# Ordering small TensorE products behind later dense products in a two-layer hybrid decoder: state-space last blocks and factors, delta-rule state updates and value transposes

## Chip, cores and metric

One Trainium2 chip, of which this kernel uses one core. The metric is the device time of the whole kernel in microseconds (us). Before the change three runs gave 2291.3 to 2293.06 us, with a median of 2291.31 us.

## What is computed

Two decoder layers over 512 tokens of width 1024, all in float32. Each layer projects the normalised input once, feeds three branches from it, and merges them:

```
y_ssd = ssd_mixer(ssd_z, ssd_xbc, ssd_dt, ...)          # 2 groups of 8 heads, blocks of 128 tokens
y_mla = mla_mixer(mla_cq, mla_ckv, mla_kr, ...)
y_gdn = gdn_mixer(gdn_qkv, gdn_z, gdn_b, gdn_a, ...)    # 8 value heads, state 128 x 128 each
mixed = g_ssd * (y_ssd @ w_ssd_out) + g_mla * (y_mla @ w_mla_out) + g_gdn * (y_gdn @ w_gdn_out)
h = x + mixed @ w_out
x = h + square(relu(rmsnorm(h) @ w_up)) @ w_down
```

Two parts matter here. The state-space mixer ends with `y * silu(z)` and an RMSNorm over the 512 channels of a group, so every token needs the sum of squares of its group before it gets a factor. The gated delta rule walks over the tokens block by block with a running state:

```
v_new = u - w @ state
o     = (q * exp(g)) @ state + qk @ v_new
state = state * exp(g_last) + (k * exp(g_last - g)).T @ v_new
```

## The kernel before

**Dense products.** Everything large is a product of 128x128 weights with 128x512 activations. An fp32 operand is split into a high and a low half, and `mm3` (L200 to L202) issues three matmuls for each product: high by high, and the two mixed ones. Weights arrive by DMA as `wraw` (two buffers), ScalarE casts them to `whi` (L172) and VectorE subtracts to get `wlo` (L173). `dense_F` runs over pairs of weight tiles k = 0..7 and over two output halves j = 0, 1, so one half-product of k is three matmuls; it accumulates in the PSUM banks called `acc`. Smaller products and transposes use three PSUM banks called `sm`, and one bank called `yt`.

**What sets the order.** Each engine runs its instructions in one fixed order, which a scheduler makes at build time. The kernel steers it with a pair of functions. `dense_F` registers every half-product under a key, `place((tag, k, j), end)`; `behind(key, ins)` puts a small product `ins` after that dense half-product. It is an order on TensorE only, without a semaphore. A key is, for example, `((ly, 1, 2 * g, "y"), 6, 0)`: in layer ly, branch 1 (latent attention), pair 2g of its output projection, the "y" half (attention output times its weights; "g" is the gate half before it), k = 6, j = 0.

**State-space group.** `ssd_group(g)` is built ahead of the output projection of latent attention for pairs 2g and 2g + 1, and its small products lie between those dense ones. For each token block t = 0..3 there are eight products of head width 64 (L784), for t > 0 four with the running state (L795), then VectorE adds (L788, L796, L797), multiplies by the gate (L811), ScalarE squares (L813), VectorE folds the squares (L814, L815), and one 128x1 product sums them over the partitions into the bank `yt` (L816). After t = 3 the factor is made: L277 on VectorE, a power on GpSimd (L278), a transpose on TensorE (L820), a copy (L822), and two DMAs through DRAM that spread it over the partitions (L823, L825). L829 multiplies it in.

**Delta-rule unit.** `gdn_unit(u)` does four heads; u = 0 runs while the projections of unit 1 go on, that is the keys `(ly, "k", 2)` and the values `(ly, "v", 4)` and `(ly, "v", 6)`; u = 1 runs in the output projection of the delta rule. For each token block: key by query (L1044), key by state (L1055), L1058 on VectorE, the inverse applied (L1061), VectorE's `vn` (L1066) and ScalarE's four scaled copies (L1072), the state update of two matmuls (L1075, into `pS`) followed by L1078 or L1082, then the outputs (L1085, L1092), L1093 and L1095, squares (L1101), and a norm with a power on GpSimd (L1105 to L1110, L278), multiplied in at L1113. At the end the unit's output is transposed in four pieces c (L1118) into the single bank `yt`, which L273 (ScalarE) and L274 (VectorE) read. In between lie the values: conv and SiLU (L719, L723, L281, L282), transposes (L1024) and L1025, and the keys' transposes (L1013, copied by L1014).

Of the kernel before, what the change touches and what calls it, by code (L numbers as in the profile page):

```python
# [20 lines left out]
P = 128  # L21
# [34 lines left out]
def hybrid_kernel(ctx, tc, a, out, depth=2, taps=None):  # L56
# [326 lines left out]
    for ly in range(depth):  # L383
# [350 lines left out]
        def ssd_group(g, yh, yl):  # L734
# [34 lines left out]
            for t in range(T):  # L769
# [11 lines left out]
                for c in range(4):  # L781
                    for i in range(2):
                        h = 2 * c + i
                        x = pe.matmul(py[64 * i : 64 * i + 64, c * P : (c + 1) * P], xd[:, t, h * 64 : (h + 1) * 64], e2[h // 4][:, h % 4, :], start=True, stop=True)  # L784
                        if t == 0:
                            behind(((ly, 1, 2 * g, "g"), 2, 0), x)
                y = xf[:, :, tok]
                dve.tensor_tensor(y, y, c4(py), ALU.add)  # L788
                if t > 0:
# [23 lines left out]
                act.activation(sq, zt, AF.Square)  # L813
                dve.tensor_tensor(sq[:, 0:2], sq[:, 0:2], sq[:, 2:4], ALU.add)  # L814
                dve.tensor_tensor(sq[:, 0], sq[:, 0], sq[:, 1], ALU.add)  # L815
                pe.matmul(pss[:, t : t + 1], sq[:, 0], ones[:, 0:1], start=True, stop=True)  # L816
            rs = mk(sp, [P, T], F32, "srs")
            rsq(rs, pss[:, :T], 1.0 / 512, EPS)
            ps = sm_bank()
            behind(((ly, 1, 2 * g, "y"), 6, 0), pe.transpose(ps[:T, :P], rs, ident))  # L820
            rsT = mk(br, [T, P], F32, "gk", 2)
            act.copy(rsT, ps[:T, :P])  # L822
            sync.dma_start(d_r[g].rearrange("(t p) -> t p", p=P), rsT)  # L823
# [172 lines left out]
        def gdn_unit(u, kT, ork, cc, cd, Yt, yh, yl):  # L996
# [20 lines left out]
            for i in range(2):  # L1017
                for j, pj in enumerate(dense_F(weights(w_in, O_GV + (4 * u + 2 * i) * P, 256, D), tiles(256), D, xh, xl, tag=(ly, "v", 4 * u + 2 * i))):
                    h = 2 * i + j
                    vf = mk(br, [P, S], F32, "ft4", 2)  # L1020
                    gconv_silu(pj, 8 + 4 * u + h, vf)
                    ps = sm_bank()
                    for t in range(T):
                        pe.transpose(ps[:, t * P : (t + 1) * P], vf[:, t * P : (t + 1) * P], ident)  # L1024
                    dve.tensor_tensor(v[:, :, h * P : (h + 1) * P], ps.rearrange("p (t n) -> p t n", t=T),  # L1025
                                      bc_last(ork[:, i, :], P), ALU.mult)
            silu_T(br, O_GZ + 512 * u, gz)
# [2 lines left out]
            ss = mk(sp, [P, T, 4], F32, "gos", 2)  # L1030
            g_, y_ = ((ly, 2, i // 2, "gy"[i % 2]) for i in range(2))
            seq = [(ly, "k", 2), (ly, "v", 4), (ly, "v", 6)] if u == 0 else [g_, y_, (ly, 2, 1, "g")]
            pw_place = (seq[0], 3, 0), (seq[0], 5, 1), (seq[1], 1, 0)
            pg_place = (seq[0], 5, 0), (seq[0], 7, 1)
            end_place = (seq[2], 1, 0) if u == 0 else (seq[2], 5, 0)
            st = None
            for t in range(T):
                tok = slice(t * P, (t + 1) * P)
# [29 lines left out]
                if t < T - 1:  # L1068
                    vd = mk(br, [P, 512], F32, "wk2")
                    for h in range(4):  # L1070
                        with tc.high_priority():
                            act.activation(hv(vd)[:, h], hv(pw)[:, h], AF.Copy, scale=cd[:, t, h : h + 1])  # L1072
                    pS = sm_bank()
                    for i in range(2):
                        pe.matmul(pS[:, i * 256 : (i + 1) * 256], ktok[i][:, t, :], vd[:, i * 256 : (i + 1) * 256], start=True, stop=True)  # L1075
                    sn = mk(br, [P, 512], F32, "st", 2)
                    if t == 0:
                        act.copy(sn, pS)  # L1078
                    else:
                        for h in range(4):  # L1080
                            with tc.high_priority():
                                dve.scalar_tensor_tensor(hv(sn)[:, h], hv(st)[:, h], hdec(2, t, h), hv(pS)[:, h], ALU.mult, ALU.add)  # L1082
                po = sm_bank()
                for h in range(4):
                    x = pe.matmul(po[:, h * P : (h + 1) * P], pt_[:, h, :], vn[:, h * P : (h + 1) * P], start=True, stop=True)  # L1085
                    if t == T - 1:
                        behind((seq[1], 1, 1), x)
                o = mk(br, [P, 512], F32, "wk3")
                if t > 0:
                    pq = sm_bank()  # L1090
# [370 lines left out]
```

## Time and profile before

| | |
|---|---|
| median of three runs | 2291.31 us |
| the profiled execution, its own time | 2290.89 us |
| its span in the trace | 2289.1 us |
| TensorE clock granted | 0.998 |
| GpSimd busy | 58.7 us |
| DMA, mean over the span | 107 GB/s |

Times inside the span are counted from its start. A row of the timeline gives the start, the length, engine, line and operation, the tile written, the tiles read, and how many instructions were merged; a square bracket behind it is the idle time of the engine before, with what ended it. Matmuls are pipelined and their ends are modelled, so two rows overlap; the distance from start to start is what counts. An fp32 matmul shows as two passes, so "x2" is one product and "x16" is eight. Rows of waits give the waiting engine and line, what it waited for, the total, the count and the longest.

### The profile page before, as it was taken

Reading aid. Unit: us, or ns where it says so; the run is one execution under the profiler, and the core shown is the slowest. Engines: PE = TensorE matmul, PEld = TensorE weight load, DVE = VectorE, ACT = ScalarE, POOL = GpSimd, SP = SyncE. Lnnn points to the kernel's source line nnn. Section 1 sums busy time; section 2 is a strip of 40 time slices with the busy share of each in tenths; the row PEclk is TensorE's granted clock in tenths of the full one; section 3 lists DMA queues with packets and bytes.
Section 4 is the critical chain, followed back from the end, with each engine's and each line's share of the span. In section 5 each row is a group of like instructions: output and inputs, shape, how many; then the busy total and the mean of one; then the engine's idle time right before and its main releaser. Section 6 shows DMA issues by size and latency. Waiting matters only on the chain.

```text
span 2289.1 us, 32304 instructions
## 1 busy us (share of the span) xinstructions
PE 2264.0 (99%) x11822; PEld 1866.7 (82%) x11822; DVE 1647.4 (72%) x3258; ACT 1202.8 (53%) x2508; POOL 58.7 (3%) x75
## 2 busy tenths in 40 slices
PE   9999999999999999999999999999999999999998
PEld 8888787888878888888888887878888887888886
DVE  7776567876676778767867775668757667778668
ACT  6766744333444465554657667443335435645545
POOL 0000000000000000000000000000001000000000
PEclk9999999999999999999999999999999999999999
DMA  4223633452225143233132236344422241432231
GB/s 144 81 74 102 193 102 120 123 150 76 77 74 172 59 148 111 92 109 105 52 100 78 77 104 199 96 119 140 129 76 82 65 170 52 166 108 99 89 111 47
DMA packets 220176, 244.23 MB, mean 107 GB/s; under 512 B 34272, under 2 KB 172528, under 8 KB 220016
## 3 DMA queue, kind: packets, MB, share of 16 engines
q1 hardware_dynamic: 220016, 242.16, 34.6%
q8 instruction: 93, 1.52, 0.3%
q14 instruction: 67, 0.55, 0.1%
HBM read 225.66 MB, written 11.74 MB: 104 GB/s over the span
## 4 chain that ended last, share of the span: by engine, by line
PE 91%; DVE 3%; ACT 2%; POOL 1%; DMA 1%; issue 0%; DVEq 0%; POOLq 0%; ACTq 0%; SPq 0%
PE acc L200 23%; PE acc L202 23%; PE acc L201 23%; PE sm L200 3%; PE sm L202 3%; PE sm L201 3%; DVE wlo L173 1%; PE sm L784 1%; PE sm L682 1%; PE sm L1085 1%; PE sm L1075 1%; PE yt L698 1%; ACT whi L172 1%; PE sm L662 1%; PE sm L659 0%
## 5 line engine op out<-in xcount | busy, mean ns | idle before, releaser
L173 DVE TENSOR_TENSOR wlo<-wraw,whi 128x512 fp32r<-128x512 f32 (+1 forms) x536 | 365.0, 686 | 344.0 <-ACT whi L172 333.8
L172 ACT CAST whi<-wraw 128x512 fp32r<-128x512 f32 (+1 forms) x536 | 329.5, 618 | 534.0 <-PE acc L201 367.1
L200 PE MATMUL acc<-xh,whi 128*128 128x512 f32 (+1 forms) x1344 | 524.5, 391 | 0.0
L201 PE MATMUL acc<-xl,whi 128*128 128x512 f32 (+1 forms) x1344 | 521.8, 388 | 0.0
L202 PE MATMUL acc<-xh,wlo 128*128 128x512 f32 (+1 forms) x1344 | 519.8, 387 | 0.0
L202 PEld LDWEIGHTS acc<-xh,wlo 128*128 128x128 f32 x1344 | 252.5, 188 | 48.8
L200 PEld LDWEIGHTS acc<-xh,whi 128*128 128x128 f32 x1344 | 252.5, 188 | 48.1 <-ACT xh L273 0.4
L201 PEld LDWEIGHTS acc<-xl,whi 128*128 128x128 f32 x1344 | 253.1, 188 | 47.3 <-DVE xl L274 0.7
L172 ACT CAST whi<-wr 128x512 fp32r<-128x512 f32 x168 | 104.3, 621 | 107.9 <-PE acc L201 47.7
L200 PE MATMUL acc<-yh,whi 128*128 128x512 f32 x384 | 151.5, 398 | 0.0
L201 PE MATMUL acc<-yl,whi 128*128 128x512 f32 x384 | 150.8, 393 | 0.0
L202 PE MATMUL acc<-yh,wlo 128*128 128x512 f32 x384 | 150.4, 392 | 0.0
L173 DVE TENSOR_TENSOR wlo<-wr,whi 128x512 fp32r<-128x512 f32 x168 | 113.2, 686 | 35.5 <-ACT whi L172 34.7
L723 DVE SCALAR_TENSOR_TENSOR ckl<-acc,pc,ckl 128x511 f32<-128x511 f32 (+2 forms) x168 | 121.1, 744 | 20.7 <-ACT ckl L719 13.0
L200 PEld LDWEIGHTS acc<-yh,whi 128*128 128x128 f32 x384 | 71.5, 188 | 16.7 <-ACT yh L273 2.3
L202 PEld LDWEIGHTS acc<-yh,wlo 128*128 128x128 f32 x384 | 72.2, 188 | 14.6
L201 PEld LDWEIGHTS acc<-yl,whi 128*128 128x128 f32 x384 | 72.2, 188 | 14.1
L200 PE MATMUL acc<-whi,xh 128*128 128x512 f32 (+1 forms) x208 | 79.9, 386 | 0.0
L201 PE MATMUL acc<-wlo,xh 128*128 128x512 f32 (+1 forms) x208 | 79.1, 380 | 0.0
L202 PE MATMUL acc<-whi,xl 128*128 128x512 f32 (+1 forms) x208 | 78.7, 381 | 0.0
L486 ACT ACTIVATE eE<-eE,cum 128x128 f32<-128x128 f32 x192 | 62.6, 391 | 28.6 <-DMA eE<-d_c 24.5
L1201 DVE TENSOR_TENSOR h<-h,acc 128x512 f32<-128x512 f32 x120 | 77.0, 680 | 0.1
(462 smaller groups left out, 4535.6 us busy)
## 6 DMA issues: line engine op xcount, KB each, us to landing
wraw<-in_w_in_dram SPq DMA_DIRECT2D x144, 512.0 KB, 3.6
wraw<-in_w_up_dram SPq DMA_DIRECT2D x64, 512.0 KB, 3.6
wr<-in_w_down_dram SPq DMA_DIRECT2D x32, 1024.0 KB, 5.3
eE<-d_c SPq DMA_DIRECT2D x48, 256.0 KB, 4.4
wraw<-in_w_mla_out_dram SPq DMA_DIRECT2D x16, 512.0 KB, 4.4
eE<-d_e SPq DMA_DIRECT2D x32, 256.0 KB, 3.1
wraw<-in_w_ssd_out_dram SPq DMA_DIRECT2D x16, 512.0 KB, 3.3
wraw<-in_w_gdn_out_dram SPq DMA_DIRECT2D x16, 512.0 KB, 3.4
```

Source lines behind the costliest of these rows:

```text
L172: act.copy(hi, raw)
L173: dve.tensor_tensor(lo, raw, f32(hi), ALU.subtract)
L200: pe.matmul(o, ah, bh, start=start, stop=False, skip_group_check=more)
L201: pe.matmul(o, ah, bl, start=False, stop=False, skip_group_check=more)
L202: return pe.matmul(o, al, bh, start=False, stop=stop, skip_group_check=more)
L486: act.activation(o[:, i], o[:, i], AF.Relu, scale=-1.0, bias=cum[:, t, h0 + i : h0 + i + 1])
L662: pe.matmul(o, qps[j][:, tok], kps[:, :n], start=False, stop=False)
L682: pe.transpose(ps[:, n : n + P], pn[t][:, kb * P : (kb + 1) * P], ident)
L698: pe.matmul(o, v_h, th[:, c : c + w], start=kb == 0, stop=False)
L723: dve.scalar_tensor_tensor(acc[:, d:], ps[:, : S - d], taps_[3 - d], acc[:, d:], ALU.mult, ALU.add)
L784: x = pe.matmul(py[64 * i : 64 * i + 64, c * P : (c + 1) * P], xd[:, t, h * 64 : (h + 1) * 64], e2[h // 4][:, h % 4, :], start=True, stop= ...
L1201: dve.tensor_tensor(hs_, hs_, ps[t], op)
```

## The change

Only orders are added or moved. (a) The last block's L784 products of a state-space group stand behind k = 3 of the projection 2g. (b) The sums L816 of t = 2 and t = 3 stand behind k = 3 and k = 7 there. (c) The factor's transpose L820 moves from k = 6 of that product to k = 1 of the gates of pair 2g + 1. (d) In `gdn_unit` for u = 1, the transposes of the first two value heads stand behind k = 5 of `(ly, "v", 6)`. (e) In both units the inverse's products (`pw_place`), the key-by-query products (`pg_place`) and the last outputs move to later dense products; the state updates of t = 1 and 2 get places of their own (`ps_place`); and the transposes that end unit 0 move from k = 1 to k = 7 of `(ly, "v", 6)`.

```diff
-                        if t == 0:
-                            behind(((ly, 1, 2 * g, "g"), 2, 0), x)
+                        if t in (0, T - 1):
+                            behind(((ly, 1, 2 * g, "g"), 2, 0) if t == 0 else ((ly, 1, 2 * g, "y"), 3, 0), x)
...
-                pe.matmul(pss[:, t : t + 1], sq[:, 0], ones[:, 0:1], start=True, stop=True)
+                x = pe.matmul(pss[:, t : t + 1], sq[:, 0], ones[:, 0:1], start=True, stop=True)
+                if t > 1:
+                    behind(((ly, 1, 2 * g, "y"), 4 * t - 5, 0), x)
...
-            behind(((ly, 1, 2 * g, "y"), 6, 0), pe.transpose(ps[:T, :P], rs, ident))
+            behind(((ly, 1, 2 * g + 1, "g"), 1, 0), pe.transpose(ps[:T, :P], rs, ident))
...
-                        pe.transpose(ps[:, t * P : (t + 1) * P], vf[:, t * P : (t + 1) * P], ident)
+                        x = pe.transpose(ps[:, t * P : (t + 1) * P], vf[:, t * P : (t + 1) * P], ident)
+                        if u == 1 and i == 0:
+                            behind(((ly, "v", 6), 5, j), x)
...
-            pw_place = (seq[0], 3, 0), (seq[0], 5, 1), (seq[1], 1, 0)
-            pg_place = (seq[0], 5, 0), (seq[0], 7, 1)
-            end_place = (seq[2], 1, 0) if u == 0 else (seq[2], 5, 0)
+            pw_place = (seq[0], 3, 0), (seq[0], 7, 0), (seq[1], 2, 0)
+            pg_place = (seq[0], 5, 1), (seq[1], 0, 1)
+            ps_place = (seq[0], 5, 0), (seq[1], 0, 0)
+            end_place = (seq[2], 7, 0) if u == 0 else (seq[2], 5, 0)
...
-                        pe.matmul(pS[:, i * 256 : (i + 1) * 256], ktok[i][:, t, :], vd[:, i * 256 : (i + 1) * 256], start=True, stop=True)
+                        x = pe.matmul(pS[:, i * 256 : (i + 1) * 256], ktok[i][:, t, :], vd[:, i * 256 : (i + 1) * 256], start=True, stop=True)
+                        if t > 0:
+                            behind(ps_place[t - 1], x)
...
-                        behind((seq[1], 1, 1), x)
+                        behind((seq[1], 2, 1), x)
```

In the changed kernel the same statements carry other line numbers from L818 on: L820 is there L822, L1024 is L1026, L1025 is L1029, L1075 is L1080, L1085 and L1092 are L1092 and L1099, L1110 and L1113 are L1117 and L1120, and L1118 is L1125.

**State-space group 0 of layer 0 on TensorE.** The rows are matmuls in their order, with the tile written, the tiles read and the size; L200 to L202 are dense. Here is the last block before the change:

```order
L201 MATMUL acc_3063<-yl_243_1066,whi_3066 128x512
L816 MATMUL yt_2695<-ct_75,wk_651_2839 128x1
L202 MATMUL acc_3063<-yh_242_1065,wlo_3067 128x512
L200 MATMUL acc_3062<-yh_326_1392,whi_3082 128x512
L784 MATMUL sm_2864<-eE_2844,tok_2256 64x128 x4
L795 MATMUL sm_2877<-ckh_547_2259,st_2835 128x128
L784 MATMUL sm_2864<-eE_2845,tok_2256 64x128 x4
L795 MATMUL sm_2877<-ckh_547_2259,st_2835 128x128 x3
L201 MATMUL acc_3062<-yl_327_1393,whi_3082 128x512
```

and here are the same products in the changed kernel:

```order
L201 MATMUL acc_3062<-yl_353_1493,whi_3082 128x512
L202 MATMUL acc_3062<-yh_352_1492,wlo_3083 128x512
L816 MATMUL yt_2695<-ct_75,wk_651_2839 128x1
L784 MATMUL sm_2864<-eE_2844,tok_2256 64x128 x4
L784 MATMUL sm_2864<-eE_2845,tok_2256 64x128 x4
L795 MATMUL sm_2877<-ckh_547_2259,st_2835 128x128 x4
L200 MATMUL acc_3063<-yh_326_1392,whi_3082 128x512
```

The sum of block 2 no longer interrupts the dense products by itself, and the last block's L784 and L795 are no longer mixed; the group stands five dense matmuls later.

**State update of block 1 in delta-rule unit 0, layer 0, on TensorE.** The tile kt holds the keys and wk the four scaled copies of L1072. This is the order before:

```order
L200 MATMUL acc_6296<-xh_30_158,whi_6334 128x512
L1075 MATMUL sm_6096<-wk_1284_6091,kt_5655 128x256
L1085 MATMUL sm_6104<-wk_1283_6089,eE_6069 128x128 x3
L1075 MATMUL sm_6096<-wk_1284_6091,kt_5656 128x256
L1085 MATMUL sm_6104<-wk_1283_6089,eE_6069 128x128
L1092 MATMUL sm_6110<-st_6039,ft_5500 128x256
L1092 MATMUL sm_6110<-st_6039,ft_5501 128x256
L201 MATMUL acc_6296<-xl_38_166,whi_6334 128x512
```

and this is it in the changed kernel:

```order
L200 MATMUL acc_6296<-xh_30_158,whi_6334 128x512
L201 MATMUL acc_6296<-xl_38_166,whi_6334 128x512
L202 MATMUL acc_6296<-xh_30_158,wlo_6335 128x512
L200 MATMUL acc_6296<-xh_31_159,whi_6334 128x512
L201 MATMUL acc_6296<-xl_39_167,whi_6334 128x512
L202 MATMUL acc_6296<-xh_31_159,wlo_6335 128x512
L1080 MATMUL sm_6096<-wk_1284_6091,kt_5655 128x256
L1080 MATMUL sm_6096<-wk_1284_6091,kt_5656 128x256
L1092 MATMUL sm_6104<-wk_1283_6089,eE_6069 128x128 x4
```

The update stands five dense matmuls later, and its second half now follows the first directly instead of after three products of L1085.

**End of unit 0 in layer 0 on VectorE.** The tile gms is the norm's factor, tok_5670 the unit's output, yt_6266 its first transposed piece. Before, the queue reads:

```order
L1110 SCALAR_TENSOR_TENSOR gms_6256<-gms_6256,grt_6253 128x4
L1025 TENSOR_TENSOR tok_6411<-sm_6505,gork_4558 128x4x128
L1113 SCALAR_TENSOR_TENSOR tok_5670<-tok_5670,gms_6256,wk_1321_6236 128x128 x4
L1105 TENSOR_SCALAR grt_6868<-grq_6395 128x2 x2
L274 SCALAR_TENSOR_TENSOR yl_1159_5492<-yt_6266,pc_122,yh_1151_5484 128x512
L173 TENSOR_TENSOR wlo_6650<-wraw_6647,whi_6649 128x512
```

and in the changed kernel:

```order
L1117 SCALAR_TENSOR_TENSOR gms_6256<-gms_6256,grt_6253 128x4
L1120 SCALAR_TENSOR_TENSOR tok_5670<-tok_5670,gms_6256,wk_1321_6236 128x128 x4
L1029 TENSOR_TENSOR tok_6411<-sm_6491,gork_4558 128x4x128
L1112 TENSOR_SCALAR grt_6868<-grq_6395 128x2 x2
L173 TENSOR_TENSOR wlo_6650<-wraw_6647,whi_6649 128x512
L1029 TENSOR_TENSOR tok_6411<-sm_6505,gork_4558 128x4x128
L723 SCALAR_TENSOR_TENSOR ckl_1391_6582<-acc_6511,pc_122,ckl_1391_6582 128x511
L274 SCALAR_TENSOR_TENSOR yl_1159_5492<-yt_6266,pc_122,yh_1151_5484 128x512
```

Between the output's last multiplication and the L274 that reads the first piece there are now five entries (two of them L1029, one wlo, one L723) where there was one.

## The prediction

> **What bounds the kernel now.** I read the page first.
>
> ```profile
> span 2289.1 us, 32304 instructions
> PE 2264.0 (99%) x11822; PEld 1866.7 (82%) x11822; DVE 1647.4 (72%) x3258; ACT 1202.8 (53%) x2508; POOL 58.7 (3%) x75
> PEclk9999999999999999999999999999999999999999
> PE 91%; DVE 3%; ACT 2%; POOL 1%; DMA 1%; issue 0%; DVEq 0%; POOLq 0%; ACTq 0%; SPq 0%
> ```
>
> TensorE is the bound: 99% busy, 91% of the chain that ended last, clock full in every slice. The change neither adds nor removes a product, so it can only win back TensorE's waits and its switches between dense and small products; and it loses wherever a product is put ahead of its operands. The view of waits gives the waits at the lines that are moved.
>
> ```profile
> PE sm L1075 <- ACT wk L1072: 3.1, 4, 0.8
> PE yt L816 <- DVE wk L815: 1.1, 4, 0.5
> PE sm L1024 <- DVE ft L282: 1.0, 2, 0.5
> PE yt L1118 <- DVE tok L1113: 0.7, 2, 0.3
> ```
>
> These 12 waits sum to 5.9 us. That is too little, because an idle time counts only from the modelled end of the matmul before. So next I read start-to-start distances in the timeline.
>
> **State-space part, worked out.** Group 0 of layer 0; first the sum and block of t = 2, then those of t = 3, then the factor.
>
> ```profile
> 243.55 1.09 PE L784 MATMUL sm<-eE,tok 128*64 128x128 f32 x16
> 245.49 0.48 PE L200 MATMUL acc<-xh,whi 128*128 128x512 f32 x1
> ...
> 246.04 0.28 PE L816 MATMUL yt<-ct,wk 128*128 128x1 f32 x2
> 246.18 0.48 PE L202 MATMUL acc<-xh,wlo 128*128 128x512 f32 x1
> 246.50 0.39 PE L200 MATMUL acc<-xh,whi 128*128 128x512 f32 x1
> ...
> 252.51 0.66 PE L784 MATMUL sm<-eE,tok 128*64 128x128 f32 x8
> 253.10 0.49 PE L795 MATMUL sm<-ckh,st 128*128 128x128 f32 x2
> 253.52 0.66 PE L784 MATMUL sm<-eE,tok 128*64 128x128 f32 x8
> 254.11 0.94 PE L795 MATMUL sm<-ckh,st 128*128 128x128 f32 x6
> 254.80 0.48 PE L201 MATMUL acc<-yl,whi 128*128 128x512 f32 x1
> ...
> 259.22 0.39 PE L202 MATMUL acc<-yh,wlo 128*128 128x512 f32 x1
> 259.45 0.39 PE L200 MATMUL acc<-yh,whi 128*128 128x512 f32 x1
> 260.06 0.35 PE L816 MATMUL yt<-ct,wk 128*128 128x1 f32 x2 [0.22 <-DVE wk L815]
> 260.27 0.48 PE L201 MATMUL acc<-yl,whi 128*128 128x512 f32 x1
> ...
> 261.28 0.40 PE L202 MATMUL acc<-yh,wlo 128*128 128x512 f32 x1
> 261.75 0.27 PE L820 MATMUL sm<-ct,srs 128*4 128x128 f32 x1
> ```
>
> A dense matmul follows the last one by 0.23 us (259.22 to 259.45). So L816 was due at 259.68 and came at 260.06, 0.38 late; its bracket shows 0.22, so 0.16 goes on top of each bracket. The unhurried L816 at 246.04 takes 0.14, the late one 0.21 (260.06 to 260.27): its load of weights lies bare, 0.07 more. The four waits of L816 in the view hold 1.1 + 4 x 0.16 + 4 x 0.07 = 2.0 us; the t = 2 sum of this group, late without a bracket, I put at 0.2, since its row reads 0.35 instead of 0.28 long. Together 2.2 us.
>
> L820 came 0.47 after the matmul ahead of it, 0.24 late; group 0 of the other layer, with the same order, I count alike: 0.5 us.
>
> The last block took 252.51 to 254.80, 2.29 us, cut in four pieces; the contiguous one at 243.55 took 1.94. With four groups, 4 x 0.35 = 1.4 us. A lone L816 costs its 0.14 and delays the next dense matmul by 0.09 (246.18 to 246.50 against 0.23); beside other small products only about half of that remains, by estimate: 4 x 0.12 = 0.5 us.
>
> Sum: 2.2 + 0.5 + 1.4 + 0.5 = **4.6 us**, if nothing is late at the new places. For group 0's last sum I checked that, with the end of L815 on VectorE:
>
> ```profile
> 259.62 0.29 DVE L815 TENSOR_TENSOR wk<-wk 128x128 f32<-128x128 f32 x1
> ```
>
> The chain from the last L795 to the end of L815 takes 259.91 - 254.80 = 5.1 us. In the new order the block ends about 0.7 us later (five dense matmuls, 1.13, less 0.35 and the lone t = 2 sum), so the sum is ready near 260.6. It is due eight dense matmuls after 259.68, less some 0.7 won by then: 260.8. That is close: 0.2 of slack, and up to 0.3 us may return at each group 0. In group 1 the last sum moves by 13 dense matmuls while its block moves by five; the eight between are 1.8 us, so it has over a microsecond. The factor leaves two microseconds later, but its reader L829 serves a product several dense stages on; SP's and VectorE's order around it moves with it, and I cost that at nothing. If that cover failed, L829 would hold up a wlo behind it.
>
> **Delta part, worked out.** First the state update of block 1 of unit 0, then of block 2.
>
> ```profile
> 592.77 1.44 POOL L278 TENSOR_TENSOR gms<-gms,nhalf 128x4 f32<-128x4 f32 x1 [46.21 <-DVE gms L277]
> ...
> 594.55 0.39 PE L200 MATMUL acc<-xh,whi 128*128 128x512 f32 x1
> ...
> 595.04 0.88 ACT L1072 ACTIVATE wk<-sm,gcd 128x128 f32<-128x128 f32 x3 [3.56 <-DVE wk L1066]
> 595.72 0.30 PEld L1075 LDWEIGHTS sm<-wk,kt 128*128 128x128 f32 x2 [1.20 <-ACT wk L1072]
> 595.72 0.70 PE L1075 MATMUL sm<-wk,kt 128*128 128x256 f32 x2 [0.78 <-ACT wk L1072]
> 595.81 0.63 ACT L172 CAST whi<-wraw 128x512 fp32r<-128x512 f32 x1
> 596.32 0.39 ACT L1072 ACTIVATE wk<-sm,gcd 128x128 f32<-128x128 f32 x1
> ...
> 604.59 0.40 PE L200 MATMUL acc<-xh,whi 128*128 128x512 f32 x1
> 604.93 0.70 PE L1075 MATMUL sm<-wk,kt 128*128 128x256 f32 x2
> ```
>
> Block 1 was due at 594.78 and came at 595.72: 0.94 late. The line's own view shows 0.10 for the bare load:
>
> ```profile
> L1075 PE MATMUL sm<-wk,kt x48: 379/380/483, 586.8 to 1822.0; 128*128 128x256 f32 x48
> ```
>
> A fast pass takes 380 ns, a late first one 483. So each wait cost 1.04 us, four times. Moved behind five dense matmuls, the update is due at 594.78 + 5 x 0.227 = 595.91, past the 595.72 at which its first half is ready. But the second half, which used to come behind three L1085, now follows at once. It reads heads 2 and 3, and a weight cast stands on ScalarE ahead of the fourth L1072, which ends at 596.71. The first half is done 0.4 later than 595.91, at 596.3: the second waits 0.4 and shows its load, 0.10. I take 0.5 back of 1.04, so 0.53 a unit, **2.1 us** for four. The bounds are 0 (a cast slipping in ahead of more copies) and 1.04.
>
> Block 2 was 0.11 late with a bare load of 0.10. In unit 1 the new place removes that: 2 x 0.23 = **0.4 us**. In unit 0 the order on ScalarE now has a weight cast (whi_6467, whose buffer comes free only when TensorE is through with the pair before) and an L719 among block 2's L1072: I take no gain there, bounds +0.8 and -0.2 a unit.
>
> [...]
>
> At the end of unit 0 the waits of the view go: L1024's 1.0 in total, L1118's 0.7, each of the four with 0.16 on top and a bare load of about 0.06, and some 0.1 a layer for the second L1024: (1.7 + 0.64 + 0.24 + 0.2) / 2 = 1.4 us a layer. What is late next is the single bank yt.
>
> ```profile
> L173 DVE TENSOR_TENSOR wlo<-wraw,whi 128x512 fp32r<-128x512 f32 (+1 forms) x536 | 365.0, 686 | 344.0 <-ACT whi L172 333.8
> 636.43 1.13 DVE L1113 SCALAR_TENSOR_TENSOR tok<-tok,gms,wk 128x128 f32<-128x128 f32 x4
> 637.20 0.69 ACT L273 ACTIVATE yh<-yt,pc 128x512 fp32r<-128x512 f32 x1 [3.46 <-PE yt L1118]
> 637.92 0.75 DVE L274 SCALAR_TENSOR_TENSOR yl<-yt,pc,yh 128x512 fp32r<-128x512 f32 x1 [0.21 <-ACT yh L273]
> ```
>
> Piece 1 may not be written before L274 has read piece 0, and in the new VectorE order L274 stands behind two L1025 (about 0.6 each from start to start), L1105 (0.25), a wlo (0.6 of its 0.686), an L723 (0.7): 2.75 us after L1113, and 3.5 with itself. Piece 1 is due nine dense matmuls (2.04) and piece 0's own 0.5 after that: 2.6. So it waits 0.9, if piece 0 came just as L1113 ended, and less the earlier L1113 is. I take 0.9: it leaves 0.5 a layer, **1.0 us**. The bounds are 1.4 a layer (VectorE ahead) and -0.8 (all four pieces each 0.5 late).
>
> **Sum.** 4.6 + 2.1 + 0.4 + 1.0 = 8.1 us. The profiled execution took 2290.89 us, so 2282.8; the median of the runs lies 0.4 above it, so I predict **2283.2**.
>
> **Rivals.**
> - *New waits replace the delta part's old ones.* For it: the second half of L1075 on the fourth L1072, the cast ahead of L1072 in unit 0, the bank yt. Against it: the first half of L1075 is clearly past its operand. Only the state-space part remains: 2291.3 - 4.6 = 2286.7.
> - *No new wait at all.* The 0.5 of each L1075 (2.0), 0.9 of each yt (1.8) and block 2 of unit 0 (0.4) come on top: 2279.0. For it speaks that VectorE and ScalarE have the same work as before and nearly the same time for it; against it, the orders worked out above, in which the second half of L1075 and piece 1 come due before their operands.
> - *The change moves waits and removes none.* The last sums land late again at group 0, and what is won is given back at the next weight cast, which already follows TensorE. Only the contiguous blocks stay, which depend on no wait: 2291.3 - 1.4 = 2289.9. Against it: three of the four kinds of wait were worked out as passed.
> - *Slower: VectorE becomes the bound at the end of unit 0.* There it runs value conv, values' norm, wlo and outputs in one queue, and it stops at L1110 for GpSimd, whose power took 1.44 us at 592.77. Bunched behind k = 5 to 7, L1113 to L274 stands in the way of the next wlo: 3.5 us and one power 1.44 exposed a layer, and the three further pieces each behind an L723 and L274 (0.7 + 0.7): 4.9 + 4.2 = 9.1 a layer, 18 in all, less the 8.1 and the 2.0 already charged for yt: 2301. From 0.56 of that exposure on (10.1 of 18) it is slower, from 0.8 on by more than 0.2%. Against it: the window there has VectorE working less than TensorE.
>
> ```profile
> 626.00:648.00 22.00, 21.17 (x106) 16.76 (x104) 19.29 (x39) 12.09 (x25) 1.01 (x1) 1.00 0.25 73
> ```
>
> The columns are TensorE, its loads, VectorE, ScalarE, GpSimd: 19.29 us of VectorE in 22, so 2.7 us of room, about one power and one wlo.
>
> **How the numbers follow.** Chances: the forecast, 2281 to 2285.5, 0.53; delta gain lost 0.2; no new wait 0.1; moved only 0.11; slower 0.06. The range takes the bounds above: with every delta bound good 2278, with every one bad and the group 0 sums 0.3 late each about 2289; I give 2279 to 2289, which leaves out the slower case, most of "moved only" and a little of the best. A measurement of this kernel tells about 0.2% (4.6 us) from no change, so faster means under 2286.7: 0.53 + 0.1 + half of 0.2 = 0.73. Within 0.2%: the other half and "moved only", 0.21. Slower 0.06.
>
> **What would show it.** State-space: no bracket at L816 and L822, blocks of 1.94 us. Delta: block 1's first half without a bracket, the second with a bracket of some 0.2 behind the fourth scaled copy (L1077 there); no wait of L1026 on L282; a wait of L1125 on L274 of about 0.7. It would be wrong if waits on wlo (L173) appear in TensorE's list near 640 or 1775, or if the last sums of group 0 wait over 0.3.

## The result, and the profile after

The changed kernel takes 2287.44 us in the median of 13 runs (2285.43 to 2288.78), the kernel before 2291.7 in 13 runs beside it: a ratio of 0.9982 with an interval of 0.9974 to 0.999. That is 4.3 us won, where 8.1 had been worked out. The profiled execution took 2287.44 us, 3.45 less than the one of before. In the views shown here and below, rows that do not matter are left out, also where no dots stand. From its page:

```profile
span 2285.6 us, 32300 instructions
PE 2261.3 (99%) x11822; PEld 1867.3 (82%) x11822; DVE 1646.9 (72%) x3258; ACT 1201.8 (53%) x2508; POOL 58.6 (3%) x75
```

TensorE is busy 2.7 us less and still bounds the kernel. The waits of TensorE at the lines in question (L1080 was L1075, L1125 was L1118):

```profile
PE sm L748 <- DVE ft L282: 1.4, 2, 1.1
PE yt L816 <- ACT eE L486: 1.3, 1, 1.3
PE sm L662 <- ACT qps L628: 1.2, 2, 0.6
...
PE sm L1080 <- ACT wk L1077: 1.0, 4, 0.3
PE yt L1125 <- DVE yl L274: 0.8, 2, 0.4
```

L1080's 3.1 us have become 1.0, L1024's 1.0 are gone, L1118's wait on L1113 has become one on the bank yt. But L748 is new to the list, L662 waits twice instead of once, and L816 holds one long wait, on another engine than before. To see which stage won what, I took the start of the same dense matmul in both traces and how much earlier it comes than in before, stage by stage; the differences over each stage are this table (us, minus is won). Runs e1 to e12 are told below; "worked out" splits the prediction's sum by stage.

| stage | worked out | after | e5 same kernel | e1 | e2 | e4 | e6 | e7 | e8 | e3 | e9 | e11 before again |
|---|---|---|---|---|---|---|---|---|---|---|---|---|
| layer 0, state-space group 0 | -1.4 | +0.37 | -1.41 | -1.33 | -0.11 | -0.66 | +1.10 | -0.29 | -1.09 | -1.41 | -1.17 | +1.01 |
| layer 0, L748 (near 298) | 0 | +1.31 | +2.84 | +2.16 | 0 | 0 | +1.96 | 0 | +1.26 | +1.00 | 0 | 0 |
| layer 0, group 1 | -0.9 | -0.86 | -0.79 | -0.86 | 0 | -0.42 | -0.86 | -0.63 | -0.77 | -0.85 | -0.40 | 0 |
| layer 0, delta unit 0 | -1.03 | -0.90 | -0.92 | 0 | -0.86 | -0.95 | -0.89 | -0.85 | -0.90 | -0.95 | -0.85 | 0 |
| layer 0, delta unit 1 | -0.73 | -0.70 | -0.73 | 0 | -0.72 | -0.74 | -0.74 | -0.72 | -0.73 | -0.74 | -0.72 | 0 |
| layer 1, L662 (near 1306) | 0 | +0.76 | +0.67 | 0 | +0.41 | +0.77 | +0.23 | +0.89 | +0.97 | +0.42 | +0.66 | 0 |
| layer 1, group 0 | -1.4 | -1.45 | -1.45 | -1.35 | +0.15 | -0.54 | +1.07 | +0.05 | -1.01 | -1.33 | -1.37 | +0.45 |
| layer 1, L748 (near 1432) | 0 | +0.33 | +0.89 | +0.53 | -0.1 | -0.1 | +0.79 | -0.1 | -0.1 | -0.1 | -0.1 | -0.1 |
| layer 1, group 1 | -0.9 | -0.91 | -0.91 | -0.91 | 0 | -0.47 | -0.91 | -0.88 | -0.59 | -0.82 | -0.91 | 0 |
| layer 1, delta units 0 and 1 | -1.76 | -1.55 | -1.61 | 0 | -1.62 | -1.56 | -1.60 | -1.52 | -1.61 | -1.56 | -1.53 | 0 |
| median against before | -8.1 | -4.3 | -5.4 | -0.7 | -3.0 | -4.8 | +1.6 | -4.1 | -5.1 | -6.9 | -6.2 | |

The column "after" sums to -3.60; 0.15 of shift ahead of the first stage makes it the 3.45 of the two executions. So every microsecond that is missing between the two profiled executions has a place: 1.75 in the state-space groups (all of it in layer 0's group 0), 1.64 at L748, 0.76 at L662, 0.35 in the delta units and those 0.15 make 4.65, which is 8.1 less 3.45. The last row holds medians and the rows above it one execution each, so the other columns need not sum to it (e5's sums to -3.42, e6's to +0.15).

**Group 0 of layer 0.** First TensorE in the changed kernel:

```profile
253.23 0.28 PE L816 MATMUL yt<-ct,wk 128*128 128x1 f32 x2
253.44 1.09 PE L784 MATMUL sm<-eE,tok 128*64 128x128 f32 x16
255.38 0.48 PE L200 MATMUL acc<-yh,whi 128*128 128x512 f32 x1
...
260.72 0.39 PE L202 MATMUL acc<-yh,wlo 128*128 128x512 f32 x1
262.38 0.35 PE L816 MATMUL yt<-ct,wk 128*128 128x1 f32 x2 [1.27 <-ACT eE L486]
```

The block (L784 and, between these rows, eight L795) takes 253.44 to 255.38, the 1.94 that was forecast, and the sum of t = 2 waits for nothing. But the last sum, due 0.23 after 260.72, comes 1.43 late. Its operand is the square L813 on ScalarE, so the next view is ScalarE's and SyncE's timeline, first of before:

```profile
251.68 0.32 SPq L484 DMA_DIRECT2D eE<-d_c  x1
253.21 1.33 SPq L484 DMA_DIRECT2D eE<-d_c  x2
256.07 1.28 ACT L486 ACTIVATE eE<-eE,cum 128x128 f32<-128x128 f32 x4 [3.10 <-DMA eE<-d_c]
258.43 0.63 ACT L813 ACTIVATE wk<-tok 128x512 f32<-128x512 f32 x1
```

and then of the changed kernel:

```profile
252.23 0.32 SPq L484 DMA_DIRECT2D eE<-d_c  x1
254.14 4.95 SPq L484 DMA_DIRECT2D eE<-d_c  x3
258.17 1.28 ACT L486 ACTIVATE eE<-eE,cum 128x128 f32<-128x128 f32 x4 [5.09 <-DMA eE<-d_c]
260.83 0.61 ACT L813 ACTIVATE wk<-tok 128x512 f32<-128x512 f32 x1
```

These L486 belong to other work: `gdn_decays` makes the delta rule's decays ahead of time in the same buffers eE (a load, exponentials L486 and L487, a store L858 to DRAM). The square stands behind them on ScalarE, and they wait for a load. (In the changed kernel the first exponential of one decay more, 0.3 us, stands ahead of it too.) That load took 4.4 us in before (251.68 to 256.07) and 5.9 here. The next loads, of which the first two take the buffers that the last block's L784 read, go out at 254.14 instead of 253.21.

**L748.** These transposes stand in the first products after the groups. SyncE and ScalarE before:

```profile
271.68 0.42 SPq L484 DMA_DIRECT2D eE<-d_c  x1
272.07 0.60 ACT L172 CAST whi<-wraw 128x512 fp32r<-128x512 f32 x1
279.62 18.67 SPq L179 DMA_DIRECT2D wraw<-in_w_in_dram  x5
```

and in the changed kernel:

```profile
273.99 0.43 SPq L484 DMA_DIRECT2D eE<-d_c  x1
274.38 0.60 ACT L172 CAST whi<-wraw 128x512 fp32r<-128x512 f32 x1
282.15 17.10 SPq L179 DMA_DIRECT2D wraw<-in_w_in_dram  x5
...
292.30 1.14 ACT L172 CAST whi<-wraw 128x512 fp32r<-128x512 f32 x2 [1.86 <-DMA wraw<-in_w_in_dram]
296.30 0.62 ACT L172 CAST whi<-wraw 128x512 fp32r<-128x512 f32 x1 [2.18 <-DMA wraw<-in_w_in_dram]
297.57 0.69 DVE L282 SCALAR_TENSOR_TENSOR ft<-ft,ckl 128x512 f32<-128x512 f32 x1
298.40 0.63 PE L748 MATMUL sm<-ct,ft 128*128 128x128 f32 x4 [1.14 <-DVE ft L282]
```

Loads, exponentials, stores, casts and weight loads of the two queues are interlocked. In the changed kernel, from 245 to 300 us, the stores L858 wait 7.2 us for exponentials (six waits), the loads of eE 9.4 us for such stores (four) and the exponentials 12.1 us for loads of eE (five), and casts and weight loads queue behind. All of it stands 2.3 to 2.5 us later than before (273.99 against 271.68, 282.15 against 279.62) although TensorE is only 0.5 later. A cast at 296.30 still waits for its weights, the SiLU L281 stands behind that cast, and L748 behind L281 and L282.

**Delta unit 0.** The state update of block 1, ScalarE and TensorE:

```profile
596.02 0.89 ACT L1077 ACTIVATE wk<-sm,gcd 128x128 f32<-128x128 f32 x3 [3.55 <-DVE wk L1071]
596.70 0.39 PEld L1080 LDWEIGHTS sm<-wk,kt 128*128 128x128 f32 x2
596.79 0.62 ACT L172 CAST whi<-wraw 128x512 fp32r<-128x512 f32 x1
596.90 0.59 PE L1080 MATMUL sm<-wk,kt 128*128 128x256 f32 x2
597.29 0.39 ACT L1077 ACTIVATE wk<-sm,gcd 128x128 f32<-128x128 f32 x1
597.73 0.30 PEld L1080 LDWEIGHTS sm<-wk,kt 128*128 128x128 f32 x2 [0.64 <-ACT wk L1077]
597.73 0.70 PE L1080 MATMUL sm<-wk,kt 128*128 128x256 f32 x2 [0.24 <-ACT wk L1077]
```

The first half waits for nothing. The second waits for the fourth scaled copy, which the cast at 596.79 pushed to 597.29: a bracket of 0.24 and, with what it hides, 0.38 late, plus 0.09 of bare load. At the end of the unit piece 1 waits for the bank yt:

```profile
640.03 0.74 DVE L274 SCALAR_TENSOR_TENSOR yl<-yt,pc,yh 128x512 fp32r<-128x512 f32 x1
640.83 0.66 PE L1125 MATMUL yt<-ct,tok 128*128 128x128 f32 x4 [0.37 <-DVE yl L274]
```

It is 0.54 late from start to start, and the last piece 0.20. One wait more is new in unit 0: the key-by-state product of block 3 (L1060, before L1055), which waited for nothing in before, comes 0.22 late behind ScalarE's copy L1100 (near 615, and 0.21 near 1748 in layer 1) and shows 0.10 of bare load.

### The profile page after: what moved, and what is told of

It is laid out like the page before. It is cut to its first block, busy times and chain, and to the rows that moved or that the text cites. A ratio compares the mean times of both kernels' runs of the same rounds, so it can differ in the third digit from the quotient of the medians.

```text
span 2285.6 us, 32300 instructions
## 1 busy us (share of the span) xinstructions
PE 2261.3 (99%) x11822; PEld 1867.3 (82%) x11822; DVE 1646.9 (72%) x3258; ACT 1201.8 (53%) x2508; POOL 58.6 (3%) x75
## 3 DMA queue, kind: packets, MB, share of 16 engines
q8 instruction: 93, 1.52, 0.3%
## 5 line engine op out<-in xcount | busy, mean ns | idle before, releaser
L200 PE MATMUL acc<-xh,whi 128*128 128x512 f32 (+1 forms) x1344 | 525.6, 392 | 0.0
L202 PE MATMUL acc<-xh,wlo 128*128 128x512 f32 (+1 forms) x1344 | 520.4, 388 | 0.0
L202 PEld LDWEIGHTS acc<-xh,wlo 128*128 128x128 f32 x1344 | 252.5, 188 | 48.8
L200 PEld LDWEIGHTS acc<-xh,whi 128*128 128x128 f32 x1344 | 252.5, 188 | 48.3 <-ACT xh L273 0.4
L200 PE MATMUL acc<-yh,whi 128*128 128x512 f32 x384 | 152.2, 400 | 0.0
L202 PE MATMUL acc<-yh,wlo 128*128 128x512 f32 x384 | 149.9, 390 | 0.0
L723 DVE SCALAR_TENSOR_TENSOR ckl<-acc,pc,ckl 128x511 f32<-128x511 f32 (+2 forms) x168 | 121.2, 744 | 17.9 <-ACT ckl L719 10.6
L200 PEld LDWEIGHTS acc<-yh,whi 128*128 128x128 f32 x384 | 71.5, 188 | 16.5 <-ACT yh L273 2.3
L202 PEld LDWEIGHTS acc<-yh,wlo 128*128 128x128 f32 x384 | 72.1, 188 | 15.1
L200 PE MATMUL acc<-whi,xh 128*128 128x512 f32 (+1 forms) x208 | 79.8, 385 | 0.0
L202 PE MATMUL acc<-whi,xl 128*128 128x512 f32 (+1 forms) x208 | 78.8, 382 | 0.0
L486 ACT ACTIVATE eE<-eE,cum 128x128 f32<-128x128 f32 x192 | 62.6, 390 | 30.9 <-DMA eE<-d_c 30.7
```

The lines of the kernel that those rows point to most:

```text
L200: pe.matmul(o, ah, bh, start=start, stop=False, skip_group_check=more)
L202: return pe.matmul(o, al, bh, start=False, stop=stop, skip_group_check=more)
L486: act.activation(o[:, i], o[:, i], AF.Relu, scale=-1.0, bias=cum[:, t, h0 + i : h0 + i + 1])
L723: dve.scalar_tensor_tensor(acc[:, d:], ps[:, : S - d], taps_[3 - d], acc[:, d:], ALU.mult, ALU.add)
```

## The experiments

The theories. **Q**: L813 is late because it queues on ScalarE behind exponentials that wait for a decay's load. **D**: the delta part gives less than worked out. **J**: the late sum of group 0 is chance. **B**: the last block, put later, holds the decay tiles eE longer, and the chain of decays pushes group 1's weights back, which makes L748 wait. **E**: the casts ahead of L748 are late because ScalarE is busy with late exponentials, not for their loads.

**e1 and e2: the two parts alone.** e1 is before with (a) to (c) of the change, e2 with (d) and (e).

> Only the state-space orders (the last block, the sums of blocks 2 and 3, the factor) on the kernel before. My prediction's term was -4.6 us. Theory Q (the part of the gain that is missing was lost on ScalarE: the squaring L813 of group 0's last block stands in the queue behind the decay exponentials L486, and these wait for a late eE load): L816 of group 0 in layer 0 waits about 1.3 us near 262, L748 waits about 1.1 us near 298, and the whole comes to -0.6 to -1.5 us. Rival D (the delta part gave less than it seems and the state-space part gave its 4.6): -4.6 us, no bracket at L816. Rival J (the late load is chance, and falls in any kernel): the waits at 262 and 298 are absent in this profile, and the time is about -4 us.

> Only the delta-rule orders (state updates, inverse products, value transposes, end of unit 0) on the kernel before. My prediction's term was -3.5 us. Theory Q: -3.1 to -3.5 us, since the state-space stage is that of before and no exponential stands ahead of a sum that TensorE waits for longer than before; the second half of the state update waits about 0.38 us and the transposes of unit 0's second piece about 0.5 us, as in the changed kernel. Rival D: near 0 to -1 us. Rival J: as Q.

e1: 2291.02 us, ratio 0.9998 (0.9989 to 1.0007). e2: 2288.72, ratio 0.9989 (0.998 to 0.9997). The delta part gives 3.2 us in its four units, 0.3 short of the working, and loses 0.41 at L662. D falls: what is missing is missing in the state-space part. There the groups give 4.45 us (1.33 + 0.86 + 1.35 + 0.91, against 4.6 worked out, and the last sum of layer 0's group 0 waits for nothing this time), and 2.69 of them go at L748.

**e3: squares first.** The exponentials of the later decays are ordered behind the last square of group 0; an order on ScalarE only.

```diff
-                act.activation(sq, zt, AF.Square)
+                last_sq[0] = act.activation(sq, zt, AF.Square).ins
...
-                act.activation(o[:, i], o[:, i], AF.Relu, scale=-1.0, bias=cum[:, t, h0 + i : h0 + i + 1])
+                x = act.activation(o[:, i], o[:, i], AF.Relu, scale=-1.0, bias=cum[:, t, h0 + i : h0 + i + 1])
+                if after:
+                    after_product(x.ins, after)
...
-                    seg_exp(e, t, 16 + 4 * u)
+                    seg_exp(e, t, 16 + 4 * u, last_sq[0] if (u, t) >= (0, 2) else None)
```

> The changed kernel with one more order on ScalarE: the exponentials of the third and later decay tiles (L486 there, from eE_2940 on) stand behind the squaring of group 0's last block, so the squaring waits for no load. Theory Q: the wait of L816 near 262 (1.43 us late in the changed kernel) falls to below 0.3, and if the wait at L748 near 298 is its consequence it falls too; time 1.4 to 2.8 us below the changed kernel, so -5.5 to -7 us against before. Rival B (the block that now stands five dense matmuls later frees the eE buffers later, and it is the loads that make everything late): the exponentials are as late, weights' casts behind them too, and the time is that of the changed kernel within 0.7. Rival J (chance): the time is that of the changed kernel, -4.3.

2284.81 us, ratio 0.9969 (0.9958 to 0.9979): the lowest median of all, 6.9 us won. The changed kernel won 4.3 in its first measurement and 5.4 in its second (e5), and the intervals overlap, so a gain over it is likely but not shown. Group 0 gives -1.41 and -1.33, no wait of the sum is left, and L748 costs 1.00 in layer 0 and nothing in layer 1. The load took 4.5 us this time, so this run did not meet a load as late as the first profile's 5.9.

**e4: the last block without its order.** The sums and the factor stay where the change puts them.

```diff
-                        if t in (0, T - 1):
-                            behind(((ly, 1, 2 * g, "g"), 2, 0) if t == 0 else ((ly, 1, 2 * g, "y"), 3, 0), x)
+                        if t == 0:
+                            behind(((ly, 1, 2 * g, "g"), 2, 0), x)
```

> The changed kernel without the order of the last block's L784 (they stand five dense matmuls earlier again, split in four pieces); everything else as changed. Rival B: the eE loads come about 0.9 us earlier, L813 too, so L816's wait near 262 goes from 1.4 to below 0.4; time -4 to -5 us against before, the 1.4 us of contiguous blocks being lost and the wait won. Theory Q: L813 still stands behind the exponentials of eE_2940, whose load waits for a store of eE_2924 and not for the block; the wait stays above 1 us whenever that load lands late, and the time is about 1.4 us above the changed kernel: -2.5 to -3 us.

2286.95 us, ratio 0.9983 (0.9975 to 0.9992). L748 waits in neither layer, so it is the block's place that brings that wait. But the four groups give 2.09 us instead of e5's 4.56, so the block's place is worth 2.5 us too, and these are given up with it. About 1.4 of them are the split blocks (four times 0.35); for most of the rest, L784 at its old place now comes ahead of its operand and waits for VectorE's L779 at both groups 0, 0.7 us by the list of waits.

**e5: the changed kernel once more**, unchanged, for what a second profile shows.

> The changed kernel once more, for a second profile. By the runs so far two losses are mixed: L816 of group 0 in layer 0 was 1.43 us late in the first profile, but not in the state-space orders alone, where the same eE load landed 4.3 us after its issue instead of 5.9. Theory Q+B (the wait at L816 hangs on when one load lands, which varies; the wait at L748 near 298 comes from the order and is there each time): L748 waits 0.8 to 1.9 us again, L816 may or may not. Rival J (both are chance): neither, and the stage 275 to 300 costs nothing. Rival Q alone (both follow from the late squares): with no wait at L816 there is none at L748. Time near 2287.4.

2286.6 us in 10 runs, ratio 0.9976 (0.9967 to 0.9985). The last sum of layer 0's group 0 does not wait: the load took 3.9 us (issued at 252.16, exponentials at 256.08) instead of 5.9, and the stage gives the whole 1.41. Since TensorE is then earlier, L748 waits longer: 2.7 us instead of 1.4. Some of what one stage wins the next gives back.

**e6: the decays' DMAs on GpSimd's queue**, so that no weight load stands behind them on SyncE: in `seg_exp` and `gdn_decays`, `sync.dma_start` becomes `pool.dma_start` for the delta rule's decays.

> The changed kernel with the decay tiles' loads and stores (16 loads of eE and 16 stores to d_e) issued by GpSimd's queue instead of SyncE's, so that no weight load stands behind them. Theory B, with the queue named (the last block frees its eE buffers later, the decay chain of load, exponentials, store and next load slips, and group 1's weight loads stand behind it on SyncE): the weight loads near 274 and 280 come at or before their old times, the wait at L748 goes; 1 to 2 us below the changed kernel, -5.5 to -6.5 against before, unless GpSimd's own issue costs more. Rival E (the late casts come from ScalarE, busy with late exponentials, not from the loads): the wait at L748 stays above 0.8 us.

2293.54 us, ratio 1.0003 (0.9994 to 1.0012), some 7 us more than the changed kernel run beside it (e5). The profile shows only about half of that (3.6 us by the table), since it is of the fastest of its eleven executions, 2290.17 us. The last sum of group 0 waits in both layers, L748 still does, and the factor's transpose too, in TensorE's waits:

```profile
PE yt L816 <- ACT eE L486: 2.5, 2, 1.3
PE sm L822 <- POOL srs L278: 1.6, 2, 0.9
PE sm L748 <- DVE ft L282: 1.5, 2, 0.8
```

and GpSimd's timeline there:

```profile
264.18 0.54 POOL L858 DMA_DIRECT2D d_e<-eE  x1
264.74 1.03 POOL L278 TENSOR_TENSOR srs<-srs,nhalf 128x4 f32<-128x4 f32 x1
```

GpSimd spends 0.54 us on this issue and 0.54 to 0.60 on the others from 250 to 276 us, and the factor's power L278 now queues behind them. And L748 waits as in the changed kernel, so SyncE's queue alone is not the cause: the casts also stand in ScalarE's queue behind the late exponentials.

**e7: five buffers for eE** instead of four (and mx, a small tile, 7 instead of 8, for the space).

```diff
-                    e = mk(br, [P, 4, P], F32, "eE", 4)
+                    e = mk(br, [P, 4, P], F32, "eE", 5)
```

> The changed kernel with five eE buffers instead of four (and seven instead of eight for the one-column tile mx, which is what the memory leaves). Theory B: a decay tile need not wait for the last block's buffer, the chain starts earlier, the wait at L748 falls below 0.3 us in both layers; -5 to -6.5 us against before. Rival E or J: L748 waits as before, and the time is that of the changed kernel.

2287.84 us, ratio 0.9977 (0.9968 to 0.9986). L748 waits in neither layer, as B says, but the time is no better than that of the changed kernel, where B had -5 to -6.5 us. With a buffer more, ScalarE's order has one more decay ahead of the square, and the last sum of group 0 waits in both layers:

```profile
258.97 0.40 ACT L486 ACTIVATE eE<-eE,cum 128x128 f32<-128x128 f32 x1 [3.87 <-DMA eE<-d_c]
...
260.39 0.62 ACT L813 ACTIVATE wk<-tok 128x512 f32<-128x512 f32 x1
...
261.94 0.35 PE L816 MATMUL yt<-ct,wk 128*128 128x1 f32 x2 [0.59 <-DVE wk L815]
```

That is theory Q again: the exponentials wait for a load, and the square behind them is late.

**e8: the last block in between**, behind k = 2 instead of k = 3.

```diff
-((ly, 1, 2 * g, "y"), 3, 0), x)
+((ly, 1, 2 * g, "y"), 2, 0), x)
```

> The changed kernel with the last block behind k = 2 instead of k = 3: it is in one piece, two dense matmuls later than before the change instead of five, and the squares L813 stand ahead of the exponentials of eE_2948 again. Theory B: most of the lateness goes, the wait at L748 is below 0.5 us and the contiguous blocks (-0.35 us each) stay, so it is 1 to 2 us below the changed kernel: -5.3 to -6.5 us against before. Rival (any order of the block for itself sets off the wait): L748 waits about 1 us again, and the time is that of the changed kernel.

2286.9 us, ratio 0.9975 (0.9965 to 0.9985). L748 costs 1.26 in layer 0, as the rival says, and nothing in layer 1, as B says, but group 0 gives 0.3 to 0.4 less than in e5, in both layers. No gain over the changed kernel that these intervals show.

**e9: squares first and five buffers together**, the edits of e3 and e7.

> The changed kernel with both cures: the exponentials of the later decays stand behind the last squares of group 0 (as in e3), and the decay tiles eE have five buffers instead of four (as in e7). Theory Q + B: the squares no longer wait for a decay's load, so no wait at L816 (L820 in this kernel) of layer 0 or 1 in group 0, and the decays' buffers no longer push the weight loads of group 1 back, so no wait of the value transposes L748 (L752 here) in either layer. State-space stages then give, against before: layer 0 -1.4 and -0.8, layer 1 -1.4 and -0.9; with the delta part's -3.1 that is -7.6 us, a ratio of 0.9967 (about 2284). Rival E (the late casts come from a ScalarE that is busy with late exponentials, not from the weight loads): the exponentials are as late as in e3, so the wait of L748 comes back with 1 us or more in layer 0 in spite of the fifth buffer, and the time is that of e3 (-6.9) at best. The wait of L662 in layer 1, which has come with 0.2 to 1.0 us in most of the changed kernels and not in before, is taken as chance by both.

2286.07 us, ratio 0.9973 (0.9962 to 0.9983). Both waits are gone: the square waits only for its own operand, and L748 (L752 here) for nothing.

```profile
259.41 0.63 ACT L817 ACTIVATE wk<-tok 128x512 f32<-128x512 f32 x1 [0.46 <-DVE tok L815]
262.47 0.28 PE L820 MATMUL yt<-ct,wk 128*128 128x1 f32 x2
```

So theories Q and B between them name both waits. E is not refuted by this run: the first exponentials behind the square are as late as in e3 (259.95 against 258.78, TensorE being 0.9 later), but the last ones ahead of L748 end at 288.48 against 289.22, although TensorE is 1.1 later there, so ScalarE too is free sooner. What the runs show is that the buffers are the source; whether the lateness reaches the casts by SyncE's queue or by ScalarE's, no run parts. The stages of this profile sum to -6.4, and its median is 6.2 below before. It was expected at -7.6: layer 0's group 1 gives 0.40 instead of 0.8, and L662 takes 0.66. It does not beat e3 (the intervals overlap).

**e10: before with five buffers**, a control.

> The kernel before with five buffers for the decay tiles instead of four, and nothing of the change. A control: theory B says the fifth buffer only takes away what the change brought in, and before has no wait at L748 that it could take; so no difference, ratio 1.000 within 0.001. If the buffer is worth something by itself (1 us or more), what e7 and e9 win is not a cure of the change but a gain of its own.

2293.54 us, ratio 1.0004 (0.9996 to 1.0013). The buffer is worth nothing by itself; it only takes away what the change brings.

**e11 and e12: before, and e2, profiled a second time.**

> The kernel before, unchanged, profiled a second time, as a measure of what the stages vary by themselves. If the wait of L662 on L628 in layer 1 is chance (it came with 0.2 to 1.0 us in all eight profiles that hold the delta part, and not in the three without it), a second profile of before may show it as well. If the delta part brings it, before again has none there. In the state-space stages all theories expect the second profile within 0.3 us of the first, and no wait at L748.

> The kernel of e2 (the delta part alone), unchanged, profiled a second time. If the wait of L662 in layer 1 is chance, it is as likely to be gone as not; if the delta part brings it, it is there again with some 0.4 us. The four delta units give -0.9, -0.7, -0.9 and -0.7 again, within 0.1.

e11 took 2295.73 us (one run; the run of before beside it 2293.44) and e12 2288.35. Both groups 0 of before are slower in the second profile, by 1.01 and 0.45; the waits of L816 hold 2.4 us instead of 1.1. In layer 0, ScalarE and TensorE:

```profile
259.04 1.28 ACT L486 ACTIVATE eE<-eE,cum 128x128 f32<-128x128 f32 x4 [4.01 <-DMA eE<-d_c]
263.03 0.35 PE L816 MATMUL yt<-ct,wk 128*128 128x1 f32 x2 [1.14 <-DVE wk L815]
```

So J and Q are both right: the queue makes the sum hang on a load, and how long the load takes varies from one execution to the next (5.9 and 3.9 us in the two profiles of the changed kernel). "Within 0.3" was wrong. The delta units of e12 give -0.89, -0.74, -0.87 and -0.75, as in e2. And L662 in layer 1 waits again in e12 and not in e11: it waits in all ten profiles with the delta part and in none of the four without. That is not chance. L662 hangs on L628 on ScalarE, which reads two transfers of 128 KB (L622). ScalarE and TensorE in the changed kernel:

```profile
1305.47 1.26 ACT L628 CAST qps<-mix 64x512 fp32r<-64x512 f32 x2 [0.81 <-DMA mix<-mix]
1306.14 0.39 PE L662 MATMUL sm<-kps,qps 128*128 128x256 f32 x1 [0.62 <-ACT qps L628]
```

Its DMAs from 1300 to 1305 us; the first row has a queue's packets, MB and share of 16 engines, the second the KB of one and the median us to landing:

```profile
q8 instruction: 1, 0.02, 2.0%
...
mix<-mix SPq DMA_DIRECT2D x2, 128.0 KB, 4.1
```

and the same view of before:

```profile
q14 instruction: 1, 0.01, 0.4%
...
mix<-mix SPq DMA_DIRECT2D x2, 128.0 KB, 2.2
```

In all ten profiles with the delta part a load of instructions (queue q8) falls into these transfers, and where their landing is given it takes 3.8 to 4.3 us; in the four without, it comes some 5 us later (at 1307.0 in before, 1302.4 in the changed kernel), and they land in 2.2 to 2.6. Both kernels make 93 such loads. The traces tell what this one goes by: it comes when TensorE has started 13,758 to 13,766 of its recorded matmuls, weight loads and waits in the four profiles without the delta part, and 13,720 to 13,725 in all ten with it. TensorE has 23,829 of them in before, 256 on average for each of the 93 loads; that these are loads of TensorE's own instructions is my estimate from these counts. By them the load hangs on a place in TensorE's program, which the delta part moves by some 35 to 45 instructions; no run moved this load alone.

## Why the prediction was half right

- **The state-space sum of 4.6 "if nothing is late at the new places"** is the step that failed, and with it what was costed at nothing around it. The sum itself came out where nothing was late: 4.56 of 4.6 in e5's four groups, with blocks of 1.94 and no wait of the t = 2 sum or of L822. That it agrees so closely is partly luck, since the two groups 0 of before differ by 1.01 and 0.45 between its own two profiles. But the check of the new places followed only the last block's own chain, from L795 to L815 on VectorE, and found 0.2 of slack. It left out two things that were in the rows of before. The first is the square: L813 stands on ScalarE behind exponentials with a bracket of 3.10 on a load; so the sum hangs on a load that took 3.7 to 5.9 us. The two profiles of the changed kernel show it: the load took 5.9 us in one and 3.9 in the other, and the sum came 1.43 late and on time. In e3 and e9, which take the dependence away, the square waits for VectorE alone. The 5.1 us that the check took as the chain's own length therefore held a wait on a load. The prediction's own sign of being wrong, a last sum of group 0 that waits over 0.3, is there in the first profile's layer 0 and not in the second profile.
- **The second thing left out, the buffers:** the last block reads decay tiles whose buffers the next decays need; moved later, it holds up that chain and with it casts and weights, and L748 pays 1.6 us (2.7 to 3.7 in e1 and e5; shown by e4 and e7, which each take the wait away, and e10; the way from the buffers to the casts is read from the rows, and no run tries it by itself).
- **"SP's and VectorE's order around the factor, at nothing"**: for the factor itself that held, no wait on L829 appeared. The order that mattered around it was that of the decays, on SyncE and ScalarE.
- **State update of block 1, 0.53 each**: right. The second half waits 0.38 and shows 0.09 of load, 0.47 for the 0.5 forecast. The load stands bare again, together with its matmul at 597.73; that of the first half, which waits for nothing, starts at 596.70, 0.20 ahead of its matmul at 596.90.
- **End of unit 0**: 0.9 was forecast for yt, 0.54 and 0.20 came. Yet in the first profile unit 0 gives 0.90 and 0.81 instead of 1.03, and unit 1 0.70 and 0.74 for 0.73: the wait of L1060, 0.22 and 0.10 of load, was not in the working of unit 0.
- **The rivals.** The time, 2287.44, is nearest to the 2286.7 of the first rival, but that is luck: the rival has the delta gain lost, and the delta part kept 3.15 of its 3.5. The wait that takes the place of the ones removed did come, but in the state-space part and not where the rival put it. The range held the time because the bounds of the delta terms were wide, not because of what failed. VectorE did not become the bound: no wait on wlo appears near 640 or 1775. The 2301 of this rival does not follow from its own terms: 18 less 8.1 and 2.0 is 7.9, which gives 2299.
- **Not foreseen at all**: 0.76 at L662, where a load of instructions falls into its transfers in every profile with the delta part.

## What to carry to other kernels

When a product is ordered later, list what its operands' buffers are next used for, and follow that reuse through the load, the engine that works on it and all that queues behind on both: here a block moved by five matmuls held a shared buffer 0.9 us longer and cost a wait of 1.3 and 2.8 us some 45 us on in layer 0, in the two profiles of the changed kernel. When the slack at a new place is checked, look at the engine queue ahead of the operand's last step for a bracket on a DMA: here its landing time varied from 3.7 to 5.9 us, and a slack of 0.2 us against that is none. A change of order is best confirmed by one run that takes the new dependence away, as e3 and e7 do, and by a second profile of the same kernel, as e5 is.

## What the runs showed of the hardware

- The same load of 256 KB into eE, at the same place in layer 0, took 3.7 to 5.9 us from issue to landing over the ten profiles with four buffers and SyncE's queue; in layer 1, 3.6 to 4.2. A load of instructions (q8) lies within it in all ten in layer 0, near 255.5 to 256.6; in layer 1 it comes ahead of it, near 1378 to 1385. That fits, but when the load falls does not order the times, so it stays open.
- Where a load of instructions fell into the transfers of L622, they landed 1.2 to 2.1 us later; in the changed kernel they ended with a tail of over a microsecond at 33 GB/s or less.
- Two profiles of the same kernel differ by 1.5 us between 50 and 200 us and by 1.6 between 900 and 1200 us (e11 against before; e4 and e9 show one or the other too). A gain of a microsecond or two is read from its own stage, not from the difference of two executions.
